# Toeplitz spreads and restacking reads issued from SyncE, the spreads one per tile of the second head, and the heads' branch first in the merge

## The chip, the cores and the metric

The kernel runs on one core of a Trainium2 chip. The metric is device microseconds of one execution. Five engines run their own streams of instructions and wait for each other through semaphores: TensorE (PE, matmuls), VectorE (DVE), ScalarE (ACT), GpSimd (POOL) and SyncE (SP). A DMA is issued by an instruction in one of these streams. Here only ScalarE (lines marked ACTq) and SyncE (SPq) issue any.

## The reference, cut to what matters

Two transformer blocks over 512 tokens and 16 meta tokens, width 1024, in float32. The change lies in the token mixer of the first block, which has two branches that are merged:

```
def token_mixer(x, ...):
    h = rmsnorm(x, g_pre)
    u, q, k, v, o, gi, gf, ga, gb = jnp.split(h @ w_in, IN_SPLITS, axis=-1)
    y_a = jax.nn.gelu(s5_ssm(u, ...))                    # state-space branch, a linear recurrence
    y_a = y_a * jax.nn.sigmoid(y_a @ w_glu)
    ...
    hb = mlstm_chunkwise(q, k, v, log_i, log_f)          # four heads
    y_b = rmsnorm_per_head(hb) * jax.nn.sigmoid(o)
    merged = sigmoid(ga) * (y_a @ w_a) + sigmoid(gb) * (y_b @ w_b)
    return x + rmsnorm(merged @ w_out, g_post)
```

`s5_ssm` is `x[t] = A x[t-1] + B u[t]`, `y[t] = Re(C x[t]) + d u[t]`, with 32 groups of 16 channels and a complex state of 64.

## The kernel before, in words

Every float32 product is made of three matmuls on split operands (a high and a low part), so a projection of one 128-wide tile of `w_in` is 48 matmuls of about 0.12 us (`mm3`, line 178). A weight tile of 512 KB is fetched on SyncE's queue by `split_w` (L165) into one of three buffers `wr`; ScalarE casts it to the high part `wh` (L167) and VectorE subtracts for the low part `wl` (L168).

The tile framework fixes the order of each engine's stream when it builds the program, from a timeline that it simulates; the order in which the code emits work is its priority. Generators (`yield`) interleave streams of work by hand; `weave` takes one step of each in turn.

The state-space branch (class `Ssm`) cuts the 528 tokens into 66 chunks of 8. For each of four tiles m of 8 groups: `load_u` writes the projected input `u` to DRAM (`ud`) and reads it back restacked as `U`. `prep` builds weights for the chunk states and calls `kernel`, which computes the response inside a chunk (`kt`), writes it to DRAM (`kd`, on SyncE's queue) and reads it back spread out into a Toeplitz matrix `tm`. `inputs` puts the chunk inputs into `X[:, 0]` and copies their halves crosswise into `X[:, 1]` with two DMAs on ScalarE's queue (L752). When all four tiles are there, `recur` runs the recurrence over 64 chunks on GpSimd, three operations for each (`ra`, `rb`, `X`, L797 to L799). `intra` multiplies `tm` by `U`; it is not part of the recurrence. `back` (L813) multiplies the finished `X` by `CA`, adds the part inside the chunk (L816), restacks through DRAM (`yd`, `yt`) and applies gelu; `glu` gates it into `yah`, `yal`.

The other branch (class `Mlstm`) projects q, k, v and a gate for each of four heads (`proj`) and runs `core` for each (L978 are its scores, L991 its values). Its result is `ybh`, `ybl`. `merge(m)`, for eight output tiles, makes two gates from projections of the input (two times 48 matmuls, `sg`, before its first `yield`), and then multiplies both branches by their weights (24 matmuls each) and sums. Until `back`, PE has projections, heads and gates to do that need neither X nor each other's results. The code weaves `back` (as `side`) and the merges' gates into heads 2 and 3.

Of the kernel before, what the change touches and what calls it, by code (L numbers as in the profile page):

```python
# [22 lines left out]
G, NP, GH, NCH = 32, 64, 16, 66  # L23
# [237 lines left out]
def mixer(c):  # L261
    nc, tc, I = c.nc, c.tc, c.I
    V, A, P = nc.vector, nc.scalar, nc.gpsimd
    xh, xl = c.xh, c.xl
    with ExitStack() as ctx:
# [18 lines left out]
        ssm = Ssm(c, hp, fs, misc, dr)  # L284
# [40 lines left out]
        def proj_part(src, n=1024, a=None, b=None):  # L325
            w = c.split_w(src, n)
            ps = dense_ps()
            if a is None:
                fa = lambda k, p: xh[:, k, HEADTOK[p] : HEADTOK[p] + HF]
                fb = lambda k, p: xl[:, k, HEADTOK[p] : HEADTOK[p] + HF]  # L330
            else:
                fa, fb = (lambda k, p: a[:, k, p]), (lambda k, p: b[:, k, p])
            c.mm3([ps[:, 0, :HF], ps[:, 1, :HF]], w, n // 128, fa, fb)
            return ps
# [3 lines left out]
        ml = Mlstm(c, hp, misc, rstd, proj_full, proj_part, rst2)  # L338
# [25 lines left out]
        ssm.powers()  # L364
        first = ml.proj(1)
        ml.rows(fs2)
        for m in range(4):
            next(first, None)
            with tc.issue_after(ml.last.ins):
                ssm.ctable(m)  # L370
            with tc.issue_after(c.mm.ins):
                ssm.intra(m)
# [5 lines left out]
        ybh = bp.tile([128, 4, 2, HF], R, name="ybh")  # L378
        ybl = bp.tile([128, 4, 2, HF], R, name="ybl")
# [7 lines left out]
        yah, yal = ya[:, 0], ya[:, 1]  # L387
# [3 lines left out]
        def glu():  # L391
            yas = yield from ssm.back(yp)
            for m in range(4):
                for p in range(2):
                    t = yas[:, m, HEADTOK[p] : HEADTOK[p] + HF]
                    A.copy(yah[:, m, p], t)
                    V.tensor_sub(yal[:, m, p], t, yah[:, m, p].bitcast(F))
            yield
            for m in range(4):
                ps = proj_part(I["wglu"][m], 512, yah, yal)  # L400
                sg = yp.tile([128, 2, HF], F, name="sg", tag="sg", bufs=2)
                A.activation(sg, ps[:, :, :HF], AF.Sigmoid)
                for p, n in ((0, 256), (1, HF)):
                    t = yas[:, m, HEADTOK[p] : HEADTOK[p] + n]
                    V.tensor_mul(t, t, sg[:, p, :n])
                yield
            for m in range(4):
                for p in range(2):
                    t = yas[:, m, HEADTOK[p] : HEADTOK[p] + HF]
                    A.copy(yah[:, m, p], t)  # L410
                    V.tensor_sub(yal[:, m, p], t, yah[:, m, p].bitcast(F))

        def merge(m):
            sig = []
            for j in range(2):
                ps = proj_part(I["w1"][20 + 2 * m + j])
                own = m == 0 or m == 1 and j == 0
                sg = (gp if own else hp).tile([128, 2, HF], F, name=f"sg{j}", tag=f"sig{m}{j}" if own else "sig",
                                              bufs=1 if own else 7)
                V.tensor_mul(sg, ps[:, :, :HF], rst2)  # L420
                A.activation(sg, sg, AF.Sigmoid)
                sig.append(sg)
            yield
            for j, (a, b) in enumerate(((yah, yal), (ybh, ybl))):
                ps = proj_part(I["wab"][m, j], 512, a, b)
                V.tensor_mul(sig[j], ps[:, :, :HF], sig[j])
            P.tensor_add(sig[0], sig[0], sig[1])
            A.copy(mgh[:, m], sig[0])
            mgl[m] = hp.tile([128, 2, HF], R, name="mgl", tag="qkv", bufs=11)
            V.tensor_sub(mgl[m], sig[0], mgh[:, m].bitcast(F))  # L430

        side = glu()
        weave([ml.core(0, ybh, ybl), ml.proj(2)])
        weave([ml.core(1, ybh, ybl), ml.proj(3)])
        pipe = [merge(m) for m in range(8)]
        weave([ml.core(2, ybh, ybl)], side, pipe[:2], limit=3, skip=1)
        weave([ml.core(3, ybh, ybl)], side, pipe[2:4])
        for _ in side:
            pass
        for m in range(9):  # L440
            if 3 < m < 8:
                next(pipe[m])
            if m:
                for _ in pipe[m - 1]:
                    pass
        yctx.close()
        cctx.close()
        bctx.close()
# [44 lines left out]
def weave(gens, side=None, once=(), limit=99, skip=0):  # L493

    live, once = list(gens), list(once)
    while live or once:
        for g in list(live):
            if next(g, live) is live:
                live.remove(g)
        skip -= 1  # L500
        if side is not None and limit > 0 and skip < 0:
            next(side, None)
            limit -= 1
        if once:
            next(once.pop(0))
# [67 lines left out]
class Ssm:  # L573
# [141 lines left out]
    def load_u(self, m, u):  # L715
        nc = self.c.nc
        U = self.U[m] = self.hp.tile([128, 8, NCH], F, name="U", tag="qkv", bufs=11)
        ud = self.dr.tile([8, 128, NCH], F, name="ud", tag="ud")
        nc.scalar.dma_start(ud.rearrange("r p c -> p r c"), u)
        nc.scalar.dma_start(U.rearrange("p g c -> p (g c)"), ud.rearrange("r (h g) c -> (r h) (g c)", g=8))  # L720

    def prep(self, m):
        c, nc, ss, misc = self.c, self.c.nc, self.ss, self.misc
# [35 lines left out]
    def kernel(self, m, wt):  # L759

        c, nc, misc = self.c, self.c.nc, self.misc
        V, A = nc.vector, nc.scalar
        gs = 8 * m
        kt = self.fs2.tile([128, 8, GH], F, name="kt", tag="kt", bufs=2)
        ps = misc()
        for j in range(8):
            nc.tensor.matmul(ps[:, GH * j : GH * j + GH], wt[:, j].rearrange("p e h -> p (e h)"),
                             self.rc[:, 0, gs + j], start=True, stop=True)
        A.copy(kt.rearrange("p g h -> p (g h)"), ps[:, : 8 * GH])
        dm = self.fs2.tile([GH, 8, GH], F, name="dm")  # L770
        V.tensor_mul(dm, c.idn[:GH, :GH].unsqueeze(1).to_broadcast([GH, 8, GH]),
                     c.v("d_t", gs, 8, GH).unsqueeze(2).to_broadcast([GH, 8, GH]))
        V.tensor_add(kt[:GH], kt[:GH], dm)
        kd = self.kd[m]
        nc.sync.dma_start(bass.AP(tensor=kd.tensor, offset=kd.offset + 112,
                                  ap=[[GH, 8], [1920, GH], [240, 8], [1, GH]]), kt)
        tm = self.tm[m] = self.fs2.tile([128, 8, 128], F, name="tm", tag="tm", bufs=4)
        nc.scalar.dma_start(tm, bass.AP(tensor=kd.tensor, offset=kd.offset,
                                        ap=[[16, 8], [1920, GH], [240, 8], [1, 128]]))

    def intra(self, m):

# [793 lines left out]
@with_exitstack  # L1576
def build(ctx, tc, I, O, dbg=False, stages=3):
    c = Core(tc, ctx, I, O, dbg)
    with ExitStack() as c.fctx:
        c.pd = c.fctx.enter_context(tc.tile_pool(name="pd", bufs=2, space=PSUM))  # L1580
        c.pm = c.fctx.enter_context(tc.tile_pool(name="pm", bufs=4, space=PSUM))
        rr = mixer(c)
        if stages == 1:
            return
        ffn(c, rr)
        c.wpx = None
    if stages == 2:
        return
    with tc.tile_pool(name="apd", bufs=3, space=PSUM) as c.pd, tc.tile_pool(name="apo", bufs=1, space=PSUM) as c.po:
        attn(c)  # L1590
        mlp(c)
# [15 lines left out]
```

## Time and profile before

| | |
|---|---|
| time, median of 3 runs | 1497.08 us (1495.68 to 1497.3) |
| the profiled execution | 1497.57 us, of which the span from first to last instruction is 1495.8 us |
| TensorE busy | 1438.1 us, 96% |
| VectorE, ScalarE, GpSimd busy | 55%, 43%, 21% |
| chain that ended last, by engine | PE 80%, POOL 8%, DVE 5%, DMA 3% |

A line of a timeline gives the start in us from the span's start, the length, the engine, the line of the kernel, the operation, what it writes and reads, and in brackets how long the engine was idle before and who released it. "x8" is eight instructions merged into a line. The trace counts two matmuls for one float32 matmul of the program that is not split, so four of L813 in the program are eight in the trace. PEclk is the granted clock of TensorE, 1.00 being 2.4 GHz.

### The profile page before, as it was taken

The page shows a single profiled execution, that of the slowest core. Times are in us where ns is not written, and L with a number is a line of the kernel's source. Part 1 is how long each engine was busy: PE and PEld are TensorE (multiplying, and loading weights), DVE is VectorE, ACT ScalarE, POOL GpSimd, SP SyncE. Part 2 cuts the span into 40 slices and gives each one's busy share as a digit, 9 for nine tenths or more (in the row PEclk, how much of TensorE's full clock was granted, in tenths as well). Part 3 has the DMA queues.
Part 4 walks back from the last instruction along what each step waited for, and adds up shares of the span by engine and source line. Part 5 has one row for each costly group of instructions (what it writes and reads, how often), then busy time and mean ns, then how long its engine had stood idle before and what let it go on. Part 6 is the DMA issues. An engine that isn't in the chain of part 4 may idle for free.

```text
span 1495.8 us, 22640 instructions
## 1 busy us (share of the span) xinstructions
PE 1438.1 (96%) x9050; PEld 1298.3 (87%) x9050; DVE 821.9 (55%) x1463; ACT 640.8 (43%) x1028; POOL 311.3 (21%) x383
## 2 busy tenths in 40 slices
PE   7899967999999999999999999999998999999998
PEld 7899967999998998889888899999786888888887
DVE  8748642564528664245643668788786542344321
ACT  4345643833333433233332347777654441134310
POOL 0008882011124211001111523233354000000000
PEclk9999987999999999999999999999999999999999
DMA  5652211232432322333223133333222322222330
GB/s 176 152 101 75 71 57 50 66 99 86 155 99 61 116 92 64 107 112 94 90 69 110 48 94 113 99 106 101 84 71 71 127 94 93 96 99 99 106 120 28
DMA packets 65892, 140.32 MB, mean 94 GB/s; under 512 B 18806, under 2 KB 30454, under 8 KB 65788
## 3 DMA queue, kind: packets, MB, share of 16 engines
q1 hardware_dynamic: 47968, 126.72, 26.6%
q10 hardware_dynamic: 17820, 12.17, 3.7%
q8 instruction: 71, 1.16, 0.3%
q14 instruction: 33, 0.27, 0.1%
HBM read 128.83 MB, written 4.76 MB: 89 GB/s over the span
## 4 chain that ended last, share of the span: by engine, by line
PE 80%; POOL 8%; DVE 5%; DMA 3%; issue 2%; ACT 2%; ACTq 0%; DVEq 0%; POOLq 0%
PE fm L178 16%; PE d L178 13%; PE mp L178 12%; PE ad L178 9%; PE ad L1185 8%; PE fg L178 8%; PE ao L178 3%; PE ad L1396 3%; POOL ra L797 3%; POOL X L799 2%; POOL rb L798 2%; PE at L1306 1%; DMA ud<-u 1%; DMA kd<-kt 1%; PE as L1281 1%
## 5 line engine op out<-in xcount | busy, mean ns | idle before, releaser
L167 ACT CAST wh<-wr 128x1024 fp32r<-128x1024 f32 (+2 forms) x240 | 232.8, 971 | 561.8 <-PE d L178 105.8
L168 DVE TENSOR_TENSOR wl<-wr,wh 128x1024 fp32r<-128x1024 f32 (+2 forms) x240 | 293.4, 1224 | 209.7 <-ACT wh L167 207.7
L178 PE MATMUL d<-xh,wl 128*128 128x258 f32 (+1 forms) x576 | 121.5, 291 | 1.7 <-DVE wl L168 1.7
L178 PE MATMUL d<-xh,wh 128*128 128x258 f32 (+1 forms) x576 | 122.3, 293 | 0.0
L178 PE MATMUL d<-xl,wh 128*128 128x258 f32 (+1 forms) x576 | 119.7, 289 | 0.0
L1185 PE MATMUL ad<-wh,xh 128*128 128x256 f32 x384 | 111.6, 295 | 2.5 <-ACT wh L167 1.3
L1185 PE MATMUL ad<-wh,xl 128*128 128x256 f32 x384 | 110.8, 290 | 1.4 <-DVE xl L563 1.4
L1185 PE MATMUL ad<-wl,xh 128*128 128x256 f32 x384 | 110.5, 290 | 0.4 <-DVE wl L168 0.4
L178 PEld LDWEIGHTS d<-xh,wl 128*128 128x128 f32 x576 | 91.8, 193 | 4.5 <-issue 2.3
L178 PEld LDWEIGHTS d<-xh,wh 128*128 128x128 f32 x576 | 92.2, 195 | 2.3 <-issue 1.0
L178 PEld LDWEIGHTS d<-xl,wh 128*128 128x128 f32 x576 | 91.9, 194 | 0.4
L1108 POOL TENSOR_TENSOR gt<-gt,ga 128x512 f32<-128x512 f32 x22 | 31.6, 1436 | 267.5 <-ACT wh L167 202.8
L1185 PEld LDWEIGHTS ad<-wh,xh 128*128 128x128 f32 x384 | 74.3, 195 | 4.0 <-ACT xh L562 1.8
L1185 PEld LDWEIGHTS ad<-wh,xl 128*128 128x128 f32 x384 | 75.0, 195 | 2.6 <-DVE xl L563 2.2
L1185 PEld LDWEIGHTS ad<-wl,xh 128*128 128x128 f32 x384 | 74.7, 195 | 0.8 <-DVE wl L168 0.6
L178 PE MATMUL fg<-xh,wh 128*128 128x258 f32 x352 | 71.9, 285 | 1.9 <-ACT xh L562 1.9
L178 PE MATMUL fg<-xl,wh 128*128 128x258 f32 x352 | 71.7, 285 | 0.7 <-DVE xl L563 0.7
L178 PE MATMUL fg<-xh,wl 128*128 128x258 f32 x352 | 72.0, 285 | 0.0
L526 POOL TENSOR_TENSOR nacc<-nacc,nsq 128x512 f32<-128x512 f32 (+1 forms) x37 | 52.8, 1427 | 91.7 <-ACT nsq L522 88.2
L178 PE MATMUL fm<-xh,wh 128*128 128x512 f32 x176 | 70.4, 400 | 0.1
L178 PE MATMUL fm<-xl,wh 128*128 128x512 f32 x176 | 70.3, 400 | 0.0
L178 PE MATMUL fm<-xh,wl 128*128 128x512 f32 x176 | 70.0, 398 | 0.0
(459 smaller groups left out, 3635.7 us busy)
## 6 DMA issues: line engine op xcount, KB each, us to landing
wr<-in_wd_dram SPq DMA_DIRECT2D x48, 512.0 KB
wr<-in_wgu_dram SPq DMA_DIRECT2D x44, 512.0 KB
wr<-in_w_dram SPq DMA_DIRECT2D x36, 512.0 KB
wr<-in_wup_dram SPq DMA_DIRECT2D x32, 512.0 KB
wr<-in_wqkv_dram SPq DMA_DIRECT2D x24, 512.0 KB
wr<-in_wo_dram SPq DMA_DIRECT2D x10, 512.0 KB
wr<-in_wab_dram SPq DMA_DIRECT2D x16, 256.0 KB
wr<-in_wd_dram SPq DMA_DIRECT2D x16, 192.0 KB
```

The costliest lines, as they stand in the source:

```text
L167: nc.scalar.copy(hi[:, :n], raw[:, :n])
L168: (eng or nc.vector).tensor_sub(lo[:, :n], raw[:, :n], hi[:, :n].bitcast(F))
L178: self.mm = self.nc.tensor.matmul(o, a[:, k, :], x(k, p), start=first and k == order[0] and t == 0, stop=last and k == order[-1] and t == 2)
L526: self.eng.tensor_add(self.parts[0], self.parts[0], sq)
L797: P.tensor_tensor(a, self.AR, X[:, :, :, k - 1].unsqueeze(1).to_broadcast([128, 2, 2, G]), op=OP.mult)
L798: P.tensor_tensor(b, a[:, 0], a[:, 1, ::-1], op=OP.add)
L799: P.tensor_tensor(X[:, :, :, k], X[:, :, :, k], b, op=OP.add)
L1108: P.tensor_mul(t, t, a)
L1185: nc.tensor.matmul(o, x[:, k, 128 * tt : 128 * tt + 128], w[:, k4], start=k == 0 and i == 0 and tt % 2 == 0, stop=k == 7 and i == 2, skip_ ...
L1281: nc.tensor.matmul(ps[:, b:e], q, kl[:, :n], start=False, stop=True, skip_group_check=True)
L1306: nc.tensor.transpose(pt[:, e : e + 128], p[:, off[i] + 128 * j : off[i] + 128 * j + 128], c.idn)
L1396: nc.tensor.matmul(ps, x[:, k], y[:, k, :S], start=i == 0 and t == 0, stop=i == kt - 1 and t == 2)
```

## The change

Three edits:

- The restacking read `U<-ud` and the Toeplitz spread `tm<-kd` are issued by SyncE instead of ScalarE. The spreads leave `kernel` for a method of their own, `spread(m)`, which the code calls around the steps of the second head's projection.
- `back` is woven in one step later and for two steps instead of three during head 2 (`limit=2, skip=2`), so its first step comes behind more of the merges' gates.
- `merge` multiplies the heads' branch (`ybh`) before the state-space branch (`yah`), with a `yield` before each. The heads' parts of merges 0 to 3 are emitted beside the last steps of `glu`, and the gates of merges 5 to 7 behind merges 2 to 4.

```diff
         first = ml.proj(1)
         ml.rows(fs2)
+        ssm.spread(0)
         for m in range(4):
             next(first, None)
+            if m < 3:
+                ssm.spread(m + 1)
...
-            yield
-            for j, (a, b) in enumerate(((yah, yal), (ybh, ybl))):
+            for j, a, b in ((1, ybh, ybl), (0, yah, yal)):
+                yield
                 ps = proj_part(I["wab"][m, j], 512, a, b)
...
-        weave([ml.core(2, ybh, ybl)], side, pipe[:2], limit=3, skip=1)
+        weave([ml.core(2, ybh, ybl)], side, pipe[:2], limit=2, skip=2)
         weave([ml.core(3, ybh, ybl)], side, pipe[2:4])
+        for m in range(4):
+            next(pipe[m])
+            next(side, None)
+        next(pipe[4])
         for _ in side:
             pass
-        for m in range(9):
-            if 3 < m < 8:
+        for m in range(8):
+            if m > 3:
                 next(pipe[m])
-            if m:
-                for _ in pipe[m - 1]:
-                    pass
+            for _ in pipe[m]:
+                pass
+            if 1 < m < 5:
+                next(pipe[m + 3])
...
-        nc.scalar.dma_start(U.rearrange("p g c -> p (g c)"), ud.rearrange("r (h g) c -> (r h) (g c)", g=8))
+        nc.sync.dma_start(U.rearrange("p g c -> p (g c)"), ud.rearrange("r (h g) c -> (r h) (g c)", g=8))
...
+    def spread(self, m):
+        kd = self.kd[m]
         tm = self.tm[m] = self.fs2.tile([128, 8, 128], F, name="tm", tag="tm", bufs=4)
-        nc.scalar.dma_start(tm, bass.AP(tensor=kd.tensor, offset=kd.offset,
-                                        ap=[[16, 8], [1920, GH], [240, 8], [1, 128]]))
+        self.c.nc.sync.dma_start(tm, bass.AP(tensor=kd.tensor, offset=kd.offset,
+                                           ap=[[16, 8], [1920, GH], [240, 8], [1, 128]]))
```

What it moves in the built program, in three places. The lines of the changed kernel stand a few lines lower: L778 became L789, L752 L760, L978 L989, L813 L824.

ScalarE's stream around the last tile of the state-space inputs, before:

```order
L769 COPY kt<-m 128x128
L736 COPY ws<-m 128x512 x2
L750 COPY X<-m 128x264 x2
L778 DMA tm<-kd 128x8x128
L752 DMA X<-X 64x528 x2
L750 COPY X<-m 128x264 x2
L899 COPY Ac<-m 128x16
```

and now:

```order
L777 COPY kt<-m 128x128
L744 COPY ws<-m 128x512 x2
L758 COPY X<-m 128x264 x2
L760 DMA X<-X 64x528 x2
L758 COPY X<-m 128x264 x2
L910 COPY Ac<-m 128x16
```

The spread, which waits for the write of `kd`, is gone from between the copies and swaps of X; the same holds for the three tiles ahead of it, and for the four reads `U<-ud` further up.

SyncE's stream at the four tiles, now (before, the rows `tm<-kd` were not there):

```order
L165 DMA wr<-in_w_dram 128x1024
L783 DMA kd<-kt 8x128x16
L789 DMA tm<-kd 128x8x128
L165 DMA wr<-in_w_dram 128x1024
L783 DMA kd<-kt 8x128x16
L789 DMA tm<-kd 128x8x128
L165 DMA wr<-in_w_dram 128x1024
```

Each spread stands right behind the write that it waits for, and the next weight load behind the spread. The built order puts the four spreads there although the code calls them later.

TensorE's stream up to the first product with the finished X, before:

```order
L978 MATMUL m<-q,k 128x264 x2
L978 MATMUL m<-q,k 128x400
L813 MATMUL m<-X,CA 128x65 x4
L178 MATMUL d<-xh,wh 128x258 x2
L178 MATMUL d<-xl,wh 128x258 x2
```

and now:

```order
L178 MATMUL d<-xl,wh 128x258 x2
L178 MATMUL d<-xh,wl 128x258 x2
L989 MATMUL m<-q,k 128x272
L989 MATMUL m<-q,k 128x144
L989 MATMUL m<-q,k 16x128
L824 MATMUL m<-X,CA 128x65 x4
```

Up to there TensorE's order is the same in both. The first product with X has moved behind 96 matmuls of L178 (gates of a merge) and the last three score matmuls of head 2; before, the 96 stood behind it, with a second group of four L813 ten matmuls on. The last X products (tile 3 of `back`) stand 21 matmuls later than before, counted from the same work. Behind the merge the order of TensorE is again the same up to the attention stage of the second block, where the scheduler has interleaved the same instructions in another order over some 1,770 positions.

## Rows read from the trace of the kernel before

**Rows 1.** Page: busy tenths of TensorE in 40 slices, and its granted clock.
```profile
PE   7899967999999999999999999999998999999998
...
PEclk9999987999999999999999999999999999999999
```

**Rows 2.** Timeline of TensorE from 205 us: start, length, what (idle before).
```profile
211.02 1.72 PE L978 MATMUL m<-q,k 128*128 128x264 f32 x6
234.66 1.97 PE L813 MATMUL m<-X,CA 128*128 128x65 f32 x8 [21.92 <-POOL X L799]
...
251.46 1.11 PE L813 MATMUL m<-X,CA 128*128 128x65 f32 x8
```

**Rows 3.** Instructions that touch tile X on GpSimd: min/median/max ns, first and last start.
```profile
L797 POOL TENSOR_TENSOR ra<-AR,X x64: 514/530/1525, 115.3 to 233.3; 128x128 f32<-128x128 f32 x64
```

**Rows 4.** Timeline of ScalarE and its DMA queue, 59 to 109 us.
```profile
65.69 1.18 ACTq L778 DMA_DIRECT2D tm<-kd  x1
...
68.19 0.64 ACT L921 ACTIVATE q<-cy 128x528 f32<-128x528 f32 x1
...
72.36 0.24 ACT L769 COPY kt<-m 128x128 f32<-128x128 f32 x1
...
97.67 0.72 ACT L750 COPY X<-m 128x264 f32<-128x264 f32 x2
103.93 0.65 ACTq L778 DMA_DIRECT2D tm<-kd  x1
104.67 2.34 ACTq L752 DMA_DIRECT2D X<-X  x2
107.05 0.66 ACT L750 COPY X<-m 128x264 f32<-128x264 f32 x2 [8.66 <-PE m L788]
...
108.25 0.61 ACTq L752 DMA_DIRECT2D X<-X  x1
```

**Rows 5.** Timeline of VectorE, 64 to 66 us.
```profile
64.44 0.75 DVE L920 SCALAR_TENSOR_TENSOR cy<-cv,vec,cy 128x528 f32<-128x528 f32 x1
```

**Rows 6.** Chain that ended last, in order of time: start us, us, what.
```profile
97.15 6.70 DMA kd<-kt
...
240.12 10.39 PE d L178 x86
```

**Rows 7.** Timeline of TensorE, 29 to 120 us.
```profile
31.75 0.51 PE L178 MATMUL d<-xh,wl 128*128 128x264 f32 x2 [1.67 <-DVE wl L168]
...
72.65 1.98 PE L746 MATMUL m<-U,ws 128*128 128x66 f32 x8 [4.31 <-ACT kt L769]
...
75.18 0.64 PE L178 MATMUL d<-xl,wh 128*128 128x264 f32 x2
...
79.40 0.41 PE L178 MATMUL d<-xh,wl 128*128 128x264 f32 x2
...
107.48 1.11 PE L788 MATMUL m<-U,tm 128*128 128x66 f32 x8 [1.02 <-ACT X L750]
```

**Rows 8.** Timeline of SyncE's DMA queue, 0 to 260 us.
```profile
71.06 0.33 SPq L165 DMA_DIRECT2D wr<-in_w_dram  x1
...
111.51 135.72 SPq L165 DMA_DIRECT2D wr<-in_w_dram  x15
```

**Rows 9.** Busy us of each engine in two stretches, granted clock, DMA share, GB/s.
```profile
31.75:68.20 36.45, 36.45 (x303) 36.38 (x303) 28.20 (x38) 7.94 (x11) 0.00 (x0) 1.00 0.62 151
112.20:149.60 37.40, 37.40 (x292) 35.38 (x292) 32.88 (x41) 21.74 (x35) 31.31 (x39) 1.00 0.24 75
```

**Rows 10.** Instructions that touch tile ys.
```profile
L816 DVE TENSOR_TENSOR ys<-m,Yi x8: 406/428/429, 236.7 to 275.2; 128x260 f32<-128x260 f32 x8
```

**Rows 11.** Instructions that touch tile ya: min/median/max ns, first and last start.
```profile
L178 PE MATMUL d<-ya,wh x192: 276/283/387, 291.1 to 397.0; 128*128 128x258 f32 x192
...
L397 DVE TENSOR_TENSOR ya<-yas,ya x8: 418/424/429, 275.9 to 286.1; 128x258 fp32r<-128x258 f32 x8
```

**Rows 12.** Waits of ScalarE over the first 500 us.
```profile
ACT wh L167 <- DMA ud<-u: 16.4, 3, 6.0
```

## The prediction

> **What bounds the kernel now.** I began with the page's slices. TensorE is at nine tenths or more nearly everywhere; the deep hole is in slices 5 and 6, counted from 0 (187 to 262 us), where the granted clock falls too [rows 1]. TensorE's timeline shows what is there: the scores of head 2 end at 212.74, and the first product with X (L813, in `back`) starts at 234.66, after 21.92 us of waiting for GpSimd [rows 2]. The work behind it is slow for a while. Two groups of L813 and the ten matmuls between them take from 234.66 to 240.12, 5.46 us, where two groups at 1.11 and ten matmuls at 0.121 (10.39 / 86) make 3.4 [rows 2, 6]. So the hole costs 21.9 and 2.0 us.
>
> The recurrence on GpSimd ends that wait. It starts at 115.3 [rows 3], ends at 234.6 and takes 119.3 us: X is ready 119 us after the start. What set the start is in the chain and in ScalarE's timeline. The last write of `kd` goes out at 97.15 and lands 6.70 us later [rows 6]. ScalarE has the spread `tm<-kd` next in its stream and stands from 98.39 until then, issues it at 103.93, and only then the swaps of X for tile 2 (104.67), the copies of X for tile 3 (107.05, after 8.66 us without work) and their swaps, the last at 108.25 [rows 4]. The recurrence waited for a transfer that it does not need.
>
> **The change part by part.**
>
> *Spreads off ScalarE.* Three effects on the start of the recurrence.
>
> (a) The last spread's wait. ScalarE goes from the copies (done at 98.39) straight to the swaps that it issued at 104.67: 6.3 us earlier.
>
> (b) The first spread's wait. ScalarE issued that spread at 65.69, began the activation for q at 68.19, and came to the copy of `kt` at 72.36 [rows 4], for which TensorE had stood 4.31 us [rows 7]. VectorE's last step ahead of q ends at 65.19 [rows 5], so q cannot begin before. I move the 4.17 us from q to the copy to there: the copy comes 3.0 us earlier, and TensorE's gap shrinks to 1.3. Behind the gap of 4.31 TensorE ran at the lower of its two clocks (1.2 of 2.4 GHz), 0.64 us for a pair of matmuls at 75.18 against 0.41 at 79.40 [rows 7]; half pace over most of those 6.75 us lost 3.0. The short gap should not cost that: 1.67 us without work ended at 31.75 [rows 7], and the 36 us from there were at a clock of 1.00 throughout [rows 9]. Together 6.0 us for what follows on TensorE, ScalarE and VectorE up to the copies of X. TensorE's wait of 1.02 us at 107.48 for those copies [rows 7] goes too; for TensorE alone 7.0.
>
> (c) The landing. From the end of the last swap's issue (108.86) to the start of the recurrence it took 6.45 us, with the 512 KB of the fourth spread just ahead in the same queue. That spread is now on the other queue. No row shows a swap alone; between 0 and 3 us I take the middle, 1.5.
>
> Start: 6.3 + 6.0 + 1.5 = 13.8 us earlier, at 101.5. The bounds are 6.3, if only (a) comes through, and 16.
>
> *The recurrence itself.* Beside a busy VectorE its operations are slower: 39 GpSimd instructions in 31.31 us (0.80 each) at 112 to 150, where VectorE is busy 88% [rows 9], against 119.3 / 192 = 0.62 over the whole, and 0.53 for the median L797 [rows 3]. GpSimd comes forward by some 7 us more than VectorE and meets that much more of its work: 7 x (0.80 - 0.62) / 0.80 = 1.6. I take 2, between 0 and 4. X is ready at 234.66 - 13.8 + 2 = 222.9, bounds 219 and 230.4.
>
> *Reads `U<-ud` off ScalarE.* ScalarE stood 16.4 us for three of them [rows 12], but TensorE was busy all through 31.75 to 68.20 [rows 9], so nothing of it lies on the path: 0. If TensorE had not had that work, up to the 16.4 would be gained; the other end is that VectorE gets done earlier with what stands ahead of q, some 2 us that would add to (b).
>
> *What is queued on SyncE.* Each spread holds the weight load behind it until `kd` has landed. The first and last of the four spreads were issued at 65.69 and 103.93, when `kd` had landed [rows 4]; the next loads went out at 71.06 and 111.51 [rows 8], since VectorE had to free a buffer. So SyncE is done with the spread 4.2 and 6.9 us before the load behind it could go: 0. Without that cover, up to 6.70 each.
>
> *Steps of `back` later.* Ahead of the wait for X now stand 96 matmuls (11.6 us) and the last scores of head 2 (250.51 to 251.46, 1.0). TensorE arrives at 212.74 - 7.0 + 12.6 = 218.4 and waits until 222.9, 4.5 us instead of 21.9. I let it pay the slow clock again, 2.0.
>
> The gain is read where equal work is done. Before, TensorE had at 251.46 behind it the 96 matmuls, the scores and two groups of L813. Now it has at 222.9 all of that but the two groups (2.2). So 251.46 - 222.9 - 2.2 - 2.0 = 24.4 us.
>
> *What is late next.* From tile 3's products with X up to the first product with `ya` there were 291.1 - 275.2 = 15.9 us of other work; now it is 82 matmuls, three scores and five value products, about 12.1. The chain between them (restacking, gelu, split) ended at 286.5, 11.3 us after those products [rows 10, 11]. Its slack falls from 4.6 us to 0.8. I take a loss of 1, at most 4. Heads' branch first gives the second writing of `ya` more room, but I see no wait in the merge to win: 0. The attention stage's new order is of the same instructions: 0, and 3 us either way.
>
> Sum: 24.4 - 1 = 23.4. The profiled execution took 1497.57 (1495.8 of span, 1.8 around it), 0.5 above the median of the runs; from it 1474.2, from the median 1473.7. I say **1474 us**.
>
> **The rivals.**
>
> *No wait left.* Landing and recurrence are quicker than I think, and X is ready by 218.4. Then there is no gap and no slow clock: 251.46 - 218.4 - 2.2 = 30.9 gained, 1466. For it: 4.5 us is little beside the bounds on X. Against it: the recurrence meets more of VectorE's work.
>
> *Only the issue time is saved.* The swaps wait for the same transfers in another way: the built program gives every DMA one of a few completion semaphores in turn, and a swap of X now waits for a write of `kd` or a spread that had the same one before it. ScalarE then saves what it spent on issuing the spreads, 0.65 to 1.18 us each [rows 4], some 3.1: X ready at 231.6, gain 251.46 - 231.6 - 2.2 - 2.0 = 15.7, 1481. With nothing saved at the start at all, 12.6 and 1485. Against it: those waits are for transfers issued a tile earlier. The Trainium skill, DMA: Bandwidth & Descriptors, section Issuing engines are not separate DMA queues, says that DMAs started by any engine run on the same 16 DMA engines, and that starting them from several saves only the sequencer's time to start them. By that alone the sum would be this rival's; the trace disagrees with it as the whole of the matter, by the 8.66 us that ScalarE was without work behind the spread.
>
> *SyncE becomes the bound (slower).* Its stream now stands for eight more landings: three `ud` of 16.4 us together and a fourth like them, 22, and four `kd` of at most 6.70, 27. If weight loads had no lead, TensorE would pay those 49 us and keep the 24: 25 slower, 1522. It decides once a load lands after ScalarE is ready to cast it. Against it: the 4.2 and 6.9 us above, and three buffers.
>
> *The gain is given back at `ya`.* ScalarE's stream, with heads, gates and table loads in it, makes the chain late by more than its 0.8 us of slack. 10 us of that would leave 13, 1484.
>
> **How the numbers follow.** Forecast 60%, no wait left 15%, only the issue time 12%, given back in part 7%, no effect 2%, SyncE the bound 4%. The likeliest by itself is 1469 to 1480. From 1465, no wait left and 1 to spare, to 1485, nothing saved at the start, leaves out the slow cases and a little of the attention stage. A measurement of this kernel can tell about 0.2% (3 us) from no change: faster by more than that 93%, the same 2%, slower 5%.
>
> **What would show it.** `ra` starting at 99 to 104; no stretch of 5 us without work on ScalarE between 61 and 100; TensorE's wait for X under 8 us and its hole in slice 5 gone; the gap at 68 near 1 us with a clock of 1.00 behind it; no cast that waits for a weight load. I am wrong if `ra` starts after 110, if TensorE waits for `ya`, or if TensorE's work ahead of 210 us takes longer than before.

## The result, and the profile after

The changed kernel takes **1473.95 us** (median of 4 runs, 1473.74 to 1474.86) beside 1496.94 for the kernel before (1495.68 to 1497.30): ratio 0.9849, 95% interval 0.9832 to 0.9866. The forecast was 1474. The sum came out; several of its terms did not, and that their errors offset each other was in part luck. The profiled execution has a span of 1472.3 us, 23.5 less than before.

TensorE's slices and its clock, from the page (compare [rows 1]):

```profile
PE   7999988999999999999999899999998999999998
...
PEclk9999998999999999999999999999999999999999
```

One slice with an 8 in the clock is left of the two slow ones, and the hole in slices 5 and 6 is shallower. Lines now stand a few further down: L778 is L789, L752 L760, L797 L808, L813 L824. TensorE's timeline, start, length and what (idle before), beside [rows 2] and [rows 7]:

```profile
66.24 1.07 PE L742 MATMUL m<-idn,wt 128*128 128x128 f32 x8
67.15 1.00 PE L754 MATMUL m<-U,ws 128*128 128x66 f32 x8
...
215.18 1.19 PE L989 MATMUL m<-q,k 128*128 128x272 f32 x6
226.20 1.97 PE L824 MATMUL m<-X,CA 128*128 128x65 f32 x8 [9.83 <-POOL X L810]
...
228.50 0.63 PE L178 MATMUL d<-xl,wh 128*128 128x258 f32 x2
...
232.59 3.76 PE L1002 MATMUL m<-Vt,Pt 128*128 128x129 f32 x30
...
270.05 0.72 PE L178 MATMUL d<-ya,wh 128*128 128x258 f32 x4
```

The gap of 4.31 us ahead of the state inputs (L754, then L746) is gone altogether. The wait for X is 9.83 us, down from 21.92, but twice the forecast 4.5. The pairs of matmuls behind it take 0.63 instead of 0.41: the lower clock again (granted 0.50 from 226.20 to 232.20). The first product with `ya` comes at 270.05 instead of 291.1 [rows 11], 21.1 earlier.

Where the merge ends, the work done is the same in both kernels. Its mark here is the last product with `mgh`, the high part of the merged result: 446.3 before (first line) and 425.7 after, 20.6 us earlier.

```profile
L178 PE MATMUL d<-mgh,wh x128: 279/283/293, 400.7 to 446.3; 128*128 128x258 f32 x128
```

```profile
L178 PE MATMUL d<-mgh,wh x128: 280/283/290, 380.0 to 425.7; 128*128 128x258 f32 x128
```

What the recurrence waited for is in ScalarE's timeline (beside [rows 4]), and the recurrence itself in the instructions that touch tile X (beside [rows 3]; min/median/max ns, first and last start):

```profile
68.77 0.24 ACT L777 COPY kt<-m 128x128 f32<-128x128 f32 x1
...
91.90 0.66 ACT L758 COPY X<-m 128x264 f32<-128x264 f32 x2 [1.19 <-PE m L754]
...
92.86 0.47 ACTq L760 DMA_DIRECT2D X<-X  x1
...
99.30 0.47 ACTq L760 DMA_DIRECT2D X<-X  x1
```

```profile
L808 POOL TENSOR_TENSOR ra<-AR,X x64: 514/531/1522, 103.2 to 224.8; 128x128 f32<-128x128 f32 x64
```

The copies of the last X come at 91.90 instead of 107.05, 15.2 us earlier, more than the 12.3 forecast. Then 11.3 us pass until the recurrence starts at 103.2, where I had allowed 6.8: the last swap is issued only at 99.30, 6.4 us after the one before it. The recurrence takes 123.0 us (103.2 to 226.2), 3.6 more than before.

SyncE's queue in those microseconds:

```profile
80.49 0.60 SPq L783 DMA_DIRECT2D kd<-kt  x1
89.52 0.59 SPq L789 DMA_DIRECT2D tm<-kd  x1
90.21 1.29 SPq L165 DMA_DIRECT2D wr<-in_w_dram  x1
91.59 0.60 SPq L783 DMA_DIRECT2D kd<-kt  x1
102.80 0.59 SPq L789 DMA_DIRECT2D tm<-kd  x1
```

Each spread holds the queue until `kd` has landed. The third goes out at 89.52, a weight load right behind it, a write of `kd` behind that, and the last four swaps of X come just then: three are issued from 90.75 to 93.3, the fourth at 99.30. The transfers between 90.3 and 99.3 us (packets, MB, share of the 16 transfer engines; q1 is SyncE's queue, q10 ScalarE's):

```profile
q1 hardware_dynamic: 1140, 0.93, 68.2%
q10 hardware_dynamic: 167, 0.29, 18.2%
```

Two swaps are 160 packets (seen below), so the three that were issued by 93.3 are 240. Only 167 had been moved by 99.3. The fourth swap went out right after the third spread had landed (98.63, from the chain that ended last: start, us, what):

```profile
89.52 9.11 DMA tm<-kd
```

In six other traces with this order of transfers (`a0_after`, for one) the profile names that landing, `tm<-kd`, as what ended ScalarE's wait there. What ended GpSimd's wait is less clear from this trace alone: the profile names a VectorE operation (`cy`, L931, done at 103.06), which `ra` does not read; in `x6_weave`, `y3_dve` and `y4_wl` it names the swap `X<-X` for the same wait.

### The profile page after: what moved, and what is told of

Read it like the earlier page. It is cut to its first block, busy times and chain, and to the rows that moved or that the text cites. A ratio compares the mean times of both kernels' runs of the same rounds, so it can differ in the third digit from the quotient of the medians.

```text
span 1472.3 us, 22643 instructions
## 1 busy us (share of the span) xinstructions
PE 1433.4 (97%) x9050; PEld 1294.6 (88%) x9050; DVE 818.8 (56%) x1463; ACT 637.4 (43%) x1026; POOL 313.8 (21%) x383
## 4 chain that ended last, share of the span: by engine, by line
PE 81%; POOL 9%; DVE 4%; issue 2%; ACT 2%; DMA 2%; ACTq 0%; DVEq 0%; POOLq 0%
PE fm L178 16%; PE d L178 13%; PE mp L178 12%; PE ad L178 9%; PE ad L1196 8%; PE fg L178 8%; PE ad L1407 3%; PE ao L178 3%; POOL ra L808 3%; POOL X L810 2%; POOL rb L809 2%; PE at L1317 1%; PE as L1292 1%; PE ao L1329 1%; DVE wl L168 1%
## 5 line engine op out<-in xcount | busy, mean ns | idle before, releaser
L178 PE MATMUL d<-xh,wl 128*128 128x258 f32 (+1 forms) x576 | 121.3, 290 | 1.8 <-DVE wl L168 1.8
L178 PE MATMUL d<-xh,wh 128*128 128x258 f32 (+1 forms) x576 | 121.9, 293 | 0.0
L178 PE MATMUL d<-xl,wh 128*128 128x258 f32 (+1 forms) x576 | 119.1, 288 | 0.0
L178 PEld LDWEIGHTS d<-xh,wl 128*128 128x128 f32 x576 | 91.3, 192 | 4.9 <-issue 2.3
L178 PEld LDWEIGHTS d<-xh,wh 128*128 128x128 f32 x576 | 91.8, 194 | 2.6 <-issue 1.0
L178 PEld LDWEIGHTS d<-xl,wh 128*128 128x128 f32 x576 | 91.0, 193 | 0.4
L178 PE MATMUL fg<-xh,wh 128*128 128x258 f32 x352 | 71.8, 285 | 1.9 <-ACT xh L570 1.9
L178 PE MATMUL fg<-xl,wh 128*128 128x258 f32 x352 | 71.7, 286 | 0.7 <-DVE xl L571 0.7
L178 PE MATMUL fg<-xh,wl 128*128 128x258 f32 x352 | 71.9, 285 | 0.0
L178 PE MATMUL fm<-xh,wh 128*128 128x512 f32 x176 | 70.3, 400 | 0.1
L178 PE MATMUL fm<-xl,wh 128*128 128x512 f32 x176 | 70.3, 400 | 0.0
L178 PE MATMUL fm<-xh,wl 128*128 128x512 f32 x176 | 70.0, 397 | 0.0
```

The source lines that it names most:

```text
L178: self.mm = self.nc.tensor.matmul(o, a[:, k, :], x(k, p), start=first and k == order[0] and t == 0, stop=last and k == order[-1] and t == 2)
```

## The experiments

Twelve runs in three groups and a last one by itself, each group beside the kernel before on the same chip. The kernel before had medians of 1498.3 to 1500.6 us there, so ratios are compared. "Start" is that of `ra`, "X ready" the first product with X, "merge" the last product with `mgh`, all from the profiled execution.

### Which part brings what

The parts apart: both DMA edits (`x1_dma`), the order of the work (`x2_order`: weave and merge, no DMA edit), and each DMA edit alone (`x3_spread` the first of the two below, `x4_ureads` the second; the spreads with their method and calls as in the change).

```diff
-        nc.scalar.dma_start(tm, bass.AP(tensor=kd.tensor, offset=kd.offset,
+        self.c.nc.sync.dma_start(tm, bass.AP(tensor=kd.tensor, offset=kd.offset,
...
-        nc.scalar.dma_start(U.rearrange("p g c -> p (g c)"), ud.rearrange("r (h g) c -> (r h) (g c)", g=8))
+        nc.sync.dma_start(U.rearrange("p g c -> p (g c)"), ud.rearrange("r (h g) c -> (r h) (g c)", g=8))
```

> Only the DMA part: spreads and U reads on SyncE, TensorE's order as before. Theory A (two independent parts of one path: when X is ready, and how much of TensorE's work stands ahead of it): the recurrence starts near 103 and X is ready near 226, 8.4 us before the 234.7 of the kernel before; TensorE still waits some 20 us for it, and the time falls by 8.4 to about 1488.5. Rival B (the order of the work alone carries the gain, the start of the recurrence is worth little): within 3 us of 1497. Rival C (the DMA part carries most of it): 1480 or less.

> Only the order: back one step later and the heads' branch first, all DMAs on ScalarE as before. Theory A: X ready at 234.7 as before, TensorE comes to it 12.6 us later and waits 9.3 instead of 21.9; the first product with ya comes 12.6 us earlier. The attention stage has the changed kernel's order here, and if that order is worth the 2.9 us by which the changed kernel gained there, the time falls by 15.5 to about 1481.5; if those 2.9 us are not the order's, by 12.6 to 1484.3. Rival B: near 1474. Rival C: 1494 or more.

> Of the DMA part only the spreads on SyncE; U reads on ScalarE, TensorE's order as before. My prediction costed the U reads at nothing: then this is the run with both DMA edits within 1 us, about 1488.5, with the recurrence starting at 103 to 104. Rival: the U reads bring VectorE and ScalarE forward ahead of q, and are worth the 1 to 3 us that I left out: 1490 to 1492, recurrence at 105 to 106.

> Of the DMA part only the U reads on SyncE; spreads on ScalarE. My prediction: 0, 1497, recurrence at 115, TensorE's wait of 4.3 us for kt still there. Rival: ScalarE and VectorE come forward by 1 to 3 us and so does the recurrence: 1494 to 1496.

| run | ratio (95%) | median us | start | X ready | length | wait for X | merge |
|---|---|---|---|---|---|---|---|
| both DMA edits | 0.9904 (0.9889 to 0.9918) | 1485.63 | 101.9 | 224.0 | 122.1 | 21.4 | 436.0 |
| order alone | 0.991 (0.9895 to 0.9925) | 1486.68 | 115.4 | 239.1 | 123.7 | 9.4 | 438.7 |
| spreads alone | 0.9927 (0.9915 to 0.994) | 1488.76 | 105.4 | 226.6 | 121.2 | 20.9 | 438.9 |
| U reads alone | 0.9972 (0.9962 to 0.9983) | 1495.29 | 113.1 | 234.6 | 121.5 | 19.5 | 446.3 |

The tile X rows of these runs, in that order:

```profile
L803 POOL TENSOR_TENSOR ra<-AR,X x64: 517/532/1607, 101.9 to 222.6; 128x128 f32<-128x128 f32 x64
```

```profile
L802 POOL TENSOR_TENSOR ra<-AR,X x64: 514/532/1591, 115.4 to 237.7; 128x128 f32<-128x128 f32 x64
```

```profile
L803 POOL TENSOR_TENSOR ra<-AR,X x64: 514/530/1522, 105.4 to 225.3; 128x128 f32<-128x128 f32 x64
```

```profile
L797 POOL TENSOR_TENSOR ra<-AR,X x64: 514/530/1582, 113.1 to 233.2; 128x128 f32<-128x128 f32 x64
```

The two parts are of about the same size, 14.4 us and 13.5 us (0.0096 x 1500.6, 0.009 x 1500.6). Rivals B and C fall. Theory A stands in kind, but its 8.4 us for the DMA part was too little; by its trace X was ready 10.7 us earlier than in [rows 2]. At the merge the two parts are 10.3 and 7.6 us ahead of the kernel before; the rest of the 14.4 and the 13.5 lies behind the merge or in the chip, where I have no trace of the kernel before.

Beside the spreads the U reads are not worth 0: the start comes 3.5 us earlier, X and the end of the merge 2.6 and 2.9 us, and the medians differ by 3.1. Alone they bring the start 2.2 us forward, but the recurrence is 2.1 longer and X and the end of the merge come as in the kernel before; the 4.2 us (2.6 to 5.7) that the timed runs show for them are not located. TensorE's waits for `kt` say how (waits of TensorE to 460 us: total, times, longest; spreads alone, then U reads alone):

```profile
PE m L749 <- ACT kt L772: 1.6, 1, 1.6
```

```profile
PE m L746 <- ACT kt L769: 4.2, 3, 2.1
```

Each edit shortens the 4.31 us of [rows 7], neither ends it; with both there is no such wait. With the U reads alone ScalarE begins the activation for q at 66.93 instead of 68.19 [rows 4]. That is the other end of the bound that I had named and not taken (VectorE done some 2 us earlier).

The order alone makes the recurrence longer, though it starts when it did in [rows 3]: 123.7 us against 119.4. So the 12.6 us of work put ahead of X did not all become gain: 7.6 at the merge.

### What holds the last swap, and three neighbours

> The changed kernel once more, unchanged, beside the next three on one chip. If the two parts add up as in theory A, its ratio to the kernel before is the sum of what the DMA part (14.4 us) and the order (13.5 us) gave alone: 0.981 or 1472 for a kernel before of 1500. If it is 0.985 as in the first measurement (23 us), some 5 us of the two are counted twice or are scatter of single runs. Its trace shows how far the length of the recurrence (123.0 us in the first trace of it, 119.4 in that of the kernel before) and the attention stage (2.9 us quicker) repeat.

The changed kernel again: ratio 0.9833 (0.982 to 0.9847), 1474.48 us, 25.0 us faster than the kernel before beside it; start 102.2, length 123.4, wait for X 10.4. So the parts add up within their scatter (14.4 and 13.5 against 25.0; at the merge 10.3 and 7.6 against 20.5). The recurrence of 123 repeats. The attention stage does not. Its first product of the last stage (tile `ao`, L178) starts at 1134.0 in the first trace and 1136.4 in this one, both with the merge's last product starting at 425.7 and 425.8:

```profile
L178 PE MATMUL ao<-xh,wh x32: 389/389/478, 1134.0 to 1357.9; 128*128 128x512 f32 x32
```

```profile
L178 PE MATMUL ao<-xh,wh x32: 388/390/477, 1136.4 to 1360.3; 128*128 128x512 f32 x32
```

With the U reads alone, whose attention stage has the old order, that stage gained 2.5 us too (1157.3 to 1154.8, its merge ending as before). From the last product with `mgh` to the first with `ao` the fourteen traces take 706.1 to 711.1 us; in the old order the kernel before takes 711.0 and the U reads alone 708.5, in the new one the changed kernel 708.3 and 710.6. The 2 to 3 us come and go from run to run; no trace ties them to an order.

Next, the swaps of X issued by GpSimd, so that none shares a completion semaphore with a spread:

```diff
-            nc.scalar.dma_start(self.X[a : a + 64, 1, gs : gs + 8], self.X[b : b + 64, 0, gs : gs + 8])
+            nc.gpsimd.dma_start(self.X[a : a + 64, 1, gs : gs + 8], self.X[b : b + 64, 0, gs : gs + 8])
```

> The changed kernel with the eight swaps of X issued by GpSimd, which has nothing else to do until the recurrence; the order of every engine but those swaps is the same, and no swap shares a completion semaphore with a spread. Theory L (in the changed kernel the last swap, at 99.3, waited 6 us for the third spread, whose completion semaphore it reuses): the recurrence starts 5 to 7 us earlier, near 97, X is ready near 220, TensorE waits about 4 us instead of 9.8, and the time falls by about 6 against the changed kernel beside it. Rival D (the last swap waited for data or for the transfer engines, not for the semaphore): the start stays at 102 to 104 and the time the same within 2. Rival S (a swap issued by GpSimd takes longer to land than one of ScalarE by as much as the wait): start at 102 or later with the swaps issued at 93.

Ratio 0.9834 (0.9821 to 0.9848), the same as the changed kernel. GpSimd's timeline, and the landing of its last two swaps (KB each, us to landing):

```profile
92.23 1.03 POOL L760 DMA_DIRECT2D X<-X  x2 [0.76 <-ACT X L758]
102.26 0.61 POOL L808 TENSOR_TENSOR ra<-AR,X 128x128 f32<-128x128 f32 x1 [9.00 <-DMA X<-X]
```

```profile
X<-X POOLq DMA_DIRECT2D x2, 132.0 KB, 9.1
```

All swaps were issued by 93.3 and landed 9 us later. Theory L falls as the whole of it: without the shared semaphore the start does not move. Whether the transfers in flight or GpSimd's way of issuing take the 9 us this run cannot say. The next group bears on it: the first two swaps, behind much the same transfers, land in 6.0 us here and in 4.9 from ScalarE's queue in `y1_late`.

Then `back` one step earlier (`x6_weave`, as before the change) and one step later (`x8_skip3`, the last line):

```diff
-        weave([ml.core(2, ybh, ybl)], side, pipe[:2], limit=2, skip=2)
+        weave([ml.core(2, ybh, ybl)], side, pipe[:2], limit=3, skip=1)
...
+        weave([ml.core(2, ybh, ybl)], side, pipe[:2], limit=1, skip=3)
```

> The changed kernel with back woven in as before (one step earlier, three steps); the heads' branch stays first in the merge. Theory A: X is ready when it is in the changed kernel, TensorE comes to it 12.6 us earlier and waits about 22, and the time is 12 to 13 above that of the changed kernel beside it, the same as the run with the DMA part alone: the merge's order is worth nothing. Rival M (the merge's order gives some of the gain): 4 us or more below that.

Ratio 0.991 (0.9897 to 0.9924), 11.5 us above the changed kernel and equal to both DMA edits alone (0.9904); wait for X 21.5. The merge's order is worth nothing that shows, and all of the order's gain is `back` one step later.

> The changed kernel with back one step later still and woven in once (limit=1, skip=3). 12 matmuls and the 15 value products of head 2, 5 us, go ahead of the wait for X, and the last tile of back comes to stand 15 value products ahead of the first product with ya. Theory Y (the chain from the last product with X to ya takes 11.9 us, and has no slack left): the wait for X falls from 9.8 to about 5, and a new wait of about 8 us for ya takes its place; the time is 2 to 6 above that of the changed kernel beside it. Rival N (what stands behind the wait for X is free to move): 5 us below the changed kernel.

Ratio 0.9843 (0.983 to 0.9857), the changed kernel's own. Both theories miss: the wait for X is 4.2 us, there is no wait of 8 us for `ya`, and still the time shows no gain. TensorE at 225.9 to 235.9 us, behind the wait (busy PE, PEld, DVE, ACT, POOL; granted clock, DMA share, GB/s), here and, second, the changed kernel's second trace at 225.6 to 235.6:

```profile
225.90:235.90 10.00, 10.00 (x60) 10.00 (x61) 4.75 (x22) 0.91 (x1) 0.00 (x0) 0.69 0.20 54
```

```profile
225.60:235.60 10.00, 10.00 (x70) 9.76 (x70) 1.66 (x7) 1.84 (x11) 0.00 (x0) 0.81 0.17 48
```

Work moved from behind the wait to before it shortens the wait, but the clock behind it falls as low after 4.2 us without work as after 10.4. By the merge the run is 2.2 us ahead (last product with `mgh` at 423.6 against 425.8); the timed runs do not show it.

### The transfers in flight, and the length of the recurrence

Spreads of tiles 2 and 3 behind the last swap (`ssm.swap`), on ScalarE's queue (`y1_late`), and the same with skip=3 (`y2_late_skip3`); the spreads of tiles 0 and 1 are called earlier and keep their place on SyncE:

```diff
...
         ssm.inputs(3)
+        with tc.issue_after(ssm.swap.ins):
+            ssm.spread(2, nc.scalar)
+            ssm.spread(3, nc.scalar)
         ssm.recur()
...
```

> The changed kernel with the spreads of tiles 2 and 3 behind the last swap of X, on ScalarE's queue; the first two stay where they were, and TensorE's order is the same. Theory D (the start of the recurrence is set by the transfers in flight: from 92 to 100 us the transfer engines are 94% busy in the changed kernel, and the third spread of 512 KB, issued at 89.5, lands together with the swaps): without it the swaps land 3 to 6 us sooner, the recurrence starts at 97 to 100, X is ready at 219 to 223, and the time is 3 to 6 us below the changed kernel's 0.9833 of the kernel before, 0.979 to 0.981. Rival E (the weight load of 90.2 or the write of kd of 91.6 sets it, or something that is no transfer): start at 102 or later, ratio 0.983 to 0.984.

Ratio **0.981 (0.9797 to 0.9824), 1469.89 us**, the fastest beside `y2`. The chain of this run (start, us), the landing of the four last swaps, and tile X:

```profile
93.08 2.39 DMA X<-X
```

```profile
X<-X ACTq DMA_DIRECT2D x4, 132.0 KB, 2.3
```

```profile
L810 POOL TENSOR_TENSOR ra<-AR,X x64: 514/532/1525, 95.9 to 221.2; 128x128 f32<-128x128 f32 x64
```

Theory D's numbers came, with a start 1 us ahead of its 97 to 100: a swap lands in 2.3 us when the third spread, and the weight load and write of `kd` that SyncE held behind it, are not in flight. The load and the write had gone out at 86.94 and 88.10 here instead of 90.21 and 91.59, so the run does not separate the spread itself from what it holds back (rival E in part). (160 packets of ScalarE's queue moved from 90 to 93.7 us here: two swaps.) The start comes 6 to 7 us earlier, and the profile names the swap as what `ra` waited for; yet X is ready only 3.0 us earlier than in the changed kernel's second trace (222.6 against 225.6), since the recurrence takes 126.7.

> The run before with back one step later still (limit=1, skip=3), where the wait for X was 4.2 us with X ready at 225.9. If X is ready by 221, that wait is gone or under 1 us, and with it the stretch at the lower clock behind it (9.4 us at a mean of 0.65 in the run with skip=3): 5 to 8 us below the changed kernel, ratio 0.978 to 0.980. If the recurrence only takes longer again, as it did each time VectorE got more work beside it, X comes at 223 or later and the ratio is 0.981 or more.

Ratio 0.9807 (0.9792 to 0.9822). The wait for X is down to 1.4 us; X came at 223.1, and the time is that of the run before. The clock over the 10 us behind 1.4 us without work was still 0.83.

Over the traces the recurrence is longer where more of VectorE's work lies beside it (119.4 us beside 71.1 busy, 123.0 beside 78.5, 126.7 beside 83.4). Two runs ask which work: 40 short products added (`y3_dve`, the first piece), and ten long subtractions done twice (`y4_wl`, the second).

```diff
                 sig.append(sg)
+                if m < 2:
+                    for _ in range(10):
+                        V.tensor_mul(junk, rst2[:, 0], rst2[:, 1])
...
-        (eng or nc.vector).tensor_sub(lo[:, :n], raw[:, :n], hi[:, :n].bitcast(F))
+        for _ in range(2 if 13 <= self.wi <= 22 else 1):
+            (eng or nc.vector).tensor_sub(lo[:, :n], raw[:, :n], hi[:, :n].bitcast(F))
```

> The changed kernel with 40 products of two halves of a scale table into a scratch tile added on VectorE, by the gates of the first two merges; they change no output. Theory V (GpSimd's recurrence gets longer by what VectorE does beside it: 119.4 us beside 71.1 us of VectorE's work in the kernel before, 121.2 to 122.1 beside 73 to 77, 123.0 to 123.7 beside 78 to 80, some 0.4 us for each): the 40 add 12 to 16 us to VectorE's busy time there and 5 to 7 us to the recurrence, 128 to 130 us from start to end. Rival W (the differences are those of the chip and of single runs): 121 to 124 as before.

> The changed kernel with the subtraction for the low part of a weight tile (L168, 1.2 us alone, both inputs in SBUF) done twice for ten weight tiles that come beside the recurrence; the result is the same. It adds some 12 us to VectorE's work there, fewer than the 40 short products did (19 us, recurrence 125.8 us). Theory P (a GpSimd operation that meets a VectorE operation with two SBUF inputs waits until that one has ended, so each long one costs up to its length and short ones little): the recurrence takes 129 to 133 us. Rival Q (the length follows VectorE's busy time, whatever the operations are): 124 to 126 us. Rival W (neither; scatter): 121 to 124.

The subtractions beside the recurrence in the kernel before and in the changed kernel's second trace (busy us, mean ns):

```profile
L168 DVE TENSOR_TENSOR wl<-wr,wh 128x1024 fp32r<-128x1024 f32 x13 | 17.5, 1349 | 3.7 <-ACT wh L167 3.4
```

```profile
L168 DVE TENSOR_TENSOR wl<-wr,wh 128x1024 fp32r<-128x1024 f32 x15 | 20.0, 1333 | 4.0 <-ACT wh L167 3.6
```

VectorE's groups beside the recurrence in the two runs, each with its tile X row:

```profile
L428 DVE TENSOR_TENSOR junk<-rst 128x258 f32<-128x258 f32 x40 | 20.6, 516 | 0.2
```

```profile
L812 POOL TENSOR_TENSOR ra<-AR,X x64: 514/537/1602, 106.0 to 230.4; 128x128 f32<-128x128 f32 x64
```

```profile
L169 DVE TENSOR_TENSOR wl<-wr,wh 128x1024 fp32r<-128x1024 f32 x25 | 32.0, 1278 | 3.6 <-ACT wh L167 3.6
```

```profile
L809 POOL TENSOR_TENSOR ra<-AR,X x64: 514/530/2409, 103.2 to 234.4; 128x128 f32<-128x128 f32 x64
```

The 40 short ones, 20.6 us of work, made it 125.8 us (106.0 to 231.8), 2.4 over the 123.4; that kernel was timed once, 1480.88 us. The ten long ones, some 12 us (the changed kernel has 15 such beside it, 20.0 us), made it 132.6 (103.2 to 235.8), 9.2 more: 0.92 for each. Theories V, Q and W fall, P holds. The run with the long ones took 1484.01 us (0.9905). `y1_late` shows it operation by operation, GpSimd first, then VectorE:

```profile
97.92 0.32 POOL L811 TENSOR_TENSOR rb<-ra 128x64 f32<-128x64 f32 x1
98.32 1.57 POOL L812 TENSOR_TENSOR X<-X,rb 128x64 f32<-128x64 f32 x1
99.97 1.52 POOL L810 TENSOR_TENSOR ra<-AR,X 128x128 f32<-128x128 f32 x1
101.56 1.19 POOL L811 TENSOR_TENSOR rb<-ra 128x64 f32<-128x64 f32 x1
```

```profile
98.32 1.35 DVE L721 TENSOR_TENSOR tmp<-ssm_c,cpow 128x1152 f32<-128x1152 f32 x1
99.58 1.51 DVE L722 TENSOR_TENSOR CA<-ssm_c,pr 128x1152 f32<-128x1152 f32 x1
101.03 1.54 DVE L168 TENSOR_TENSOR wl<-wr,wh 128x1024 fp32r<-128x1024 f32 x1
```

From 98.3 to 102.7 the two engines take turns: three steps that take 0.36, 0.53 and 0.32 us alone take 1.57, 1.52 and 1.19, each about until the VectorE operation beside it is done. The Trainium skill, SBUF — State Buffer, section SBUF: two separate sides, says that VectorE and GpSimd share a pair of ports under an exclusive lock, held for a whole instruction, and that a VectorE operation with two SBUF inputs takes it against a GpSimd operation that reads SBUF. The trace agrees, with those numbers.

## Why the prediction was right, point by point

- **(a) and (b), ScalarE's waits.** Right in kind, too small: 15.2 us at the copies for 12.3. The part that failed is "U reads off ScalarE: 0". I went only by what TensorE did during the three waits; VectorE and ScalarE were late ahead of q as well. The reads are worth 2.9 us at the merge beside the spreads, and 0 there alone. Both edits together end the 4.31 us wait; the spreads alone would have left 1.6. The bound of 16 us on the start is 15.3 when (a), (b) and (c) are added, and the late bound of 230.4 on X takes 2 for the recurrence where 4 was allowed; the forecast does not hang on either.
- **(c), the landing.** The sign was wrong: forecast 1.5 us shorter, it gave back 3 us. The bound "between 0 and 3" left out that SyncE's queue, held by the third spread, sends a spread, a load and a write together just when the swaps go. "What is queued on SyncE: 0" was right for TensorE, which waited for no weights, and wrong for the transfers. The rival on shared semaphores did happen (the last swap went out at 99.30 and not at 93.3), but no price shows: the three swaps ahead of it had not landed by then either, and without the shared semaphore the start was the same (`x5_pool`, where GpSimd issues the swaps, and part of the 9 us may be its way of issuing). The Trainium skill's rule in the prediction (DMA: Bandwidth & Descriptors, section Issuing engines are not separate DMA queues) is half borne out: swaps that landed in 2.3 us in `y1_late` had not landed after 6 with the other queue's transfers in flight; that issuing from another engine saves only issue time is not what the spreads alone show (11 us, against some 3.1 of issuing).
- **Start.** 103.2 for 101.5, inside the 99 to 109.
- **The recurrence.** 2 us forecast (0 to 4), 3.6 measured. I counted only what the earlier start brings beside VectorE; with both DMA edits alone that was 2.7. The 96 matmuls moved ahead of X bring their weight tiles' subtractions as well: 13 of them beside the recurrence before, 15 now and 16 with the order alone.
- **X ready, and the wait.** 226.2 for 222.9, 9.8 us for 4.5; "under 8 us" failed. TensorE came to it at 216.4 (226.20 - 9.83), 2 earlier than forecast; 1.3 of that is what I had left of its wait for `kt`.
- **The slow clock.** 2.0 forecast. From 226.20 to 232.59 two groups of L824 and 14 matmuls ran, which at full pace are 2.2 + 14 x 0.121 = 3.9 us: 2.5.
- **Gain at the merge.** With these numbers the same formula gives 251.46 - 226.2 - 2.2 - 2.5 = 20.6. The last product of the merge with `mgh` started at 446.3 before and at 425.7 after: 20.6.
- **`ya`, loss of 1.** None was seen: TensorE did not wait for it. The step was wrong: I took the whole chain from the last X product to the first `ya` product as one. With skip=3 the first product with `ya` started at 267.1, 2.1 us behind the last restacking sum at 265.0, and only 0.3 us of waiting for `ya` showed behind it: the first products do not need the last tile.
- **Merge's order, 0.** Right (`x6_weave`).
- **Attention stage, 0 and 3 either way.** 2.9 us quicker in the profiled execution, and that made the sum meet: the gain at the merge was 3.8 short of the 24.4, and these 2.9 and the 1 not lost at `ya` filled it. That is luck, for the 2.9 are scatter: the same kernel's second trace has 2.4 less of it. The median of the second measurement was 25.0 us below its kernel before, so the gain of the change is 23 to 25 us; where the kernel before loses its extra 2 to 4 us on the other chips stays open.
- **The signs.** `ra` started at 103.2, inside the 99 to 104, and no cast waited for a weight load of this stage. The gap at 68 went altogether, and its slow clock with it. The hole in slice 5 is shallower (8 tenths) and not gone, and ScalarE still stood 5.3 us without work ahead of 99.81, around the last swap.
- **The rivals.** "SyncE the bound" and "given back at `ya`" did not happen. "No wait left" is what `y1_late` with skip=3 nearly reaches, and it is worth 4 us, not the 8 that I gave it, for the recurrence lengthens as it starts earlier and the clock fell after this wait of 1.4 us too.

## What to carry to other kernels

A wait that is taken out of one engine's stream should be followed into the stream that gets it: there it holds back other transfers, and sends them in a bunch when it ends. When work is put into a gap to fill it, ask what the engine that the gap waits for shares with that work; here each long subtraction added beside the recurrence cost it 0.92 us. Here, moving the last two spreads behind the small transfers that the recurrence needs gave 0.981 (0.9797 to 0.9824), where the changed kernel gave 0.9833 (0.982 to 0.9847) and 0.9849: some 3 us, not beside it on one chip, and the intervals meet. In the traces the merge ends at 421.6 against 425.8.

## What the runs showed of the hardware

- A GpSimd operation of 0.3 to 0.5 us lasts 1.2 to 1.6 beside a VectorE operation of 1.2 to 1.5 us on two SBUF inputs. Ten more of those cost 9.2 us; 40 of 0.5 us cost 2.4.
- A swap of 132 KB landed in 2.3 us with no spread or weight load in flight. Beside a spread and a weight load of 512 KB each, three that were issued by 93.3 had not all landed 6 us later.
- The clock behind TensorE's wait for X was low whatever the wait's length: its mean over the next 10 us was 0.76 after 21.9 us without work, 0.69 and 0.81 after 9.8 and 10.4, 0.72 after 6.5, 0.69 after 4.2 and 0.83 after 1.4. There, a wait that was shortened but not removed paid most of it. A short wait need not: TensorE's 1.67 us ahead of 31.75 in the kernel before [rows 9], and 1.58 ahead of 71.21 with the spreads alone, were followed by 1.00; 1.70 ahead of 71.40 with the U reads alone were followed by 0.87 and then 0.50.
